# Moving a gate product to the branch stage, other buffer counts in the mixers, one raw weight buffer and another spacing of the convolution pairs in a hybrid decoder layer

## The chip, the cores and the metric

The kernel runs on one core of a Trainium2 chip. A core has the engines PE (TensorE, matrix products), DVE (VectorE), ACT (ScalarE), POOL (GpSimd) and SP (SyncE), which here issues all the DMAs. Each engine runs its own list of instructions in order; semaphores make one wait for another. The metric is the device time of one launch in microseconds (us). Times come from runs, and the profile from one execution of its own.

## The reference

One layer of a decoder with four branches runs over 16 meta tokens, 1024 prompt tokens and 8 samples of 4 tokens, all in float32, 1024 wide:

```
xn = rmsnorm(h)
gq, gk, gv, glr, gg, hq, hf, hi, hg, mq, mk, mv, mi, mf, mo, mg, ca, cb, cg, gate = split(xn @ w_in)
zA = head_rmsnorm(gla(gq, gk, gv, glr)) * silu(gg)
zB = head_rmsnorm(hgrn2(hq, hf, hi))    * silu(hg)
zC = head_layernorm(mlstm(mq, mk, mv, mi, mf) * sigmoid(mo)) * silu(mg)
zD = silu(layernorm(causal_conv31(ca * sigmoid(cb)))) * silu(cg)
mixed = sum_b sigmoid(gate_b) * (z_b @ w_branch[b])
y = rmsnorm(h + mixed @ w_out)
```

Each branch is 512 wide, four heads of 128. Recurrent and convolution states are outputs too.

## The kernel before, in words

A float32 operand of a product is split into a high and a low part (`split_w`: ACT writes `wh`, L138, POOL or DVE writes `wl`, L139), and each product is three matrix products on PE: high by high, low by high, high by low. Raw weights come from HBM into the tile `wraw` (`load_raw`, L132), two buffers in the pool `wp`; `wh` and `wl` have two each.

The program is written in one order, and a planner turns it into a fixed list for each engine. It takes, at each point of a modelled time, the ready instruction that comes first in the program; a tile with all its buffers taken makes the next user wait. So a tile's number of buffers (`bufs`) decides what can run ahead, and the lists were fixed before the chip runs them.

The stages, with their rough times in the profile:

- 0 to 90 us: normalisation, transposition, the first gate projections (`gate_direct`), and sums of x for the next stage (`combine_x`).
- 90 to 500 us: 19 projection pairs. A pair computes two blocks of 128 columns of `xn @ w_in` with seven half-size products instead of eight (`pair`, L252 to L311): r0 and r1 are the two raw weights, DVE and ACT form sums of weights and of results, PE runs 7 x 24 matrix products. Four of the pairs are convolution pairs (`conv_pair`): they write u = ca * sigmoid(cb) into the tile `u`, one buffer (ACT at L349 first). `conv_taps` then runs the 31 taps on DVE (L386, L388) into `y`, one buffer, behind the transposes of the stored convolution state (PE L372, into `u` by ACT L373, small products at L383); `tc.cur_priority = pr + 700` ranks its DVE work behind that of the pairs after it. `conv_states` writes the new state out. The other 15 pairs (`pair_to`) send gates, `cg` and silu(gg), silu(hg), silu(mg), sigmoid(mo) to DRAM (`gscr`, `cscr`, `sscr`). The loop at L457 puts a convolution pair at places 0, 4, 8 and 12 of the 19.
- 500 to 1300 us: the mixers: four HGRN2 heads, two GLA units of two heads, four mLSTM heads. The products over levels of the decay are in the tile `tot`, the running states and some scratch in `sall`, one buffer each; `f` holds the decay, one buffer. 16 further gate blocks (`filler`) are projected here as work for PE. At its end each head calls `z_out` (L702): scale, transpose on PE into PSUM, and a DVE product (L720) of the PSUM result, the norm's weight and the gate, which was loaded from `sscr` into the tile `gt`; then one store to `zscr` (L721).
- 1300 to 1518 us: the branch stage, in the order b = 1, 0, 2, 3. `load_z` (L1140) loads four z of a branch and splits them, for the next branch while the current one runs (for b = 1, ahead of it). For each of eight column blocks, `branch` loads a weight (256 KB), splits it and runs 36 matrix products; DVE multiplies by the gate (L1164), POOL adds to the sum (L1165). During b = 1 the convolution's norm (`conv_norm`) runs as well.
- 1518 to 1621 us: the product with `w_out` and the last norm.

PSUM has three accumulators (`acc`), two buffers for levels and three for all else (`mm`) in the mixers and branches.

Of the kernel before, what the change touches and what calls it, by code (L numbers as in the profile page):

```python
# [12 lines left out]
F32 = mybir.dt.float32  # L13
# [3 lines left out]
AF = mybir.ActivationFunctionType  # L17
ALU = mybir.AluOpType
# [47 lines left out]
def trunk(ctx, tc, hx, w_in, w_sm, w_br, w_out, pk, wgk2, mlb, fnorm, s_gla, s_hg, s_c, s_n, s_m, s_cv,  # L66
# [43 lines left out]
    def col(name, i=0):  # L110
        return pkt[:, PK[name][0] + i:PK[name][0] + i + 1]
# [16 lines left out]

    def load_raw(src, c0, kd=KD):
        raw = pools["wp"].tile([P, KD, P], F32, name="wraw", tag="wraw")  # L130
        src = src if c0 is None else src[:, c0:c0 + P].rearrange("(k p) m -> p k m", p=P)
        DMA.dma_start(raw[:, :kd], src)  # L132
        return raw
# [118 lines left out]
    def pair(c0, c1, c11, c12, c22, c21):  # L252


        wp = pools["gph"]
        r0, r1 = load_raw(w_in, c0), load_raw(w_in, c1)
        b11, b21, b12, b22 = r0[:, :KH], r0[:, KH:], r1[:, :KH], r1[:, KH:]
# [199 lines left out]
    for i in range(4):  # L457
        cu = conv_pair(i)
        pair_to(*todo.pop(0))
        conv_taps(i, *cu)  # L460
        pair_to(*todo.pop(0))
        conv_states(i, *cu)
        pair_to(*todo.pop(0))
    for t in todo:
# [55 lines left out]
    def tl(tag, shape=None, bufs=None, name=None):  # L520
        return mx.tile(shape or [P, NT], F32, name=name or tag, tag=tag, bufs=bufs)
# [66 lines left out]
    def levels(qv, nh, k, f):  # L588

        tot = tl("tot", [P, 1072], 1)  # L590
        atts = [(nxt(attb, "att"), att8b[cnt["att"] % 2]) for _ in range(nh)]
# [109 lines left out]

    def z_out(o, rstd, nw, gate, zi, mu=None):  # L702
        if mu is not None:
            for c in range(9):
                n = csz(c)
                V.tensor_scalar(o[:n, c], o[:n, c], mu[:n, c:c + 1], rstd[:n, c:c + 1], ALU.add, ALU.mult)
        else:
            for a in (0, 4):
                V.tensor_tensor(o[:, a:a + 4], o[:, a:a + 4], rstd[:, a:a + 4].unsqueeze(2).broadcast_to([P, 4, P]),
                                ALU.mult)  # L710
            V.tensor_scalar(o[:TAIL, 8], o[:TAIL, 8], rstd[:TAIL, 8:9], None, ALU.mult)
        for c0, c1 in QUADS:
            n = csz(c0)
            ps = mmt("zt")
            for c in range(c0, c1):
                T.transpose(ps[:, (c - c0) * P:(c - c0) * P + n], o[:n, c, :], ident[:n, :n])
            a = NM if c0 == 0 else 0
            e = (c1 - c0 - 1) * P + n
            t0 = c0 * P + a - NM
            V.scalar_tensor_tensor(gate[:, t0:t0 + e - a], ps[:, a:e], nw, gate[:, t0:t0 + e - a], ALU.mult, ALU.mult)  # L720
        DMA.dma_start(zscr[zi], gate)  # L721

    def rms(os, epss):
        n = len(os)
        sq = tl("sall", [P, 9, P], 1, name="sq")
        ms = tl("ms", [P, 18], 1)
        G.memset(ms, 1.0)
        for i, o in enumerate(os):
            for a in (0, 4):
                S.activation(sq[:, a:a + 4], o[:, a:a + 4], AF.Square)  # L730
                V.tensor_reduce(ms[:, 9 * i + a:9 * i + a + 4], sq[:, a:a + 4], AX.X, ALU.add)
            S.activation(sq[:TAIL, 8], o[:TAIL, 8], AF.Square, accum_out=ms[:TAIL, 9 * i + 8:9 * i + 9])
        ms = ms[:, :9 * n]
        V.tensor_scalar(ms, ms, 1.0 / P, EPS * epss, ALU.mult, ALU.add)
        return rsqrt(ms)

    def filler():
        gate_direct(fill.pop(0), tmp=lambda: tl("gd", [P, 352], 1))

    def linear_unit(uid, qv, nh, k, f, prod, vts, s0, epss, finish, pout, sout):  # L740
# [17 lines left out]
        k9 = split3(xk, 2, "k9", 1, mmt("k9p"))  # L758
        sall = tl("sall", [P, 9, P], 1)
        for c0, c1 in QUADS:  # L760
# [60 lines left out]
    def gla_unit(p):  # L821
# [19 lines left out]
        vts = [vtok("gv", 2 * p + i) for i in range(2)]  # L841
        gates = []
        for i in range(2):
            g = tl("gt", [P, NY], 2)
            DMA.dma_start(g, sscr[2 * p + i])
            gates.append(g)
        s0 = tl("s0", [P, NSEQ, 129], 1)[:, :, 0:P]
        DMA.dma_start(s0, s_gla[:, 2 * p:2 * p + 2].rearrange("b h k v -> (h k) b v"))
        linear_unit(p, qg, 2, k, f, prod, vts, s0, 64.0,
                    lambda i, o, r: z_out(o, r, col("gla_norm"), gates[i], 2 * p + i),  # L850
                    lambda st: DMA.dma_start(p_gla[2 * p:2 * p + 2].rearrange("h k v -> (h k) v"), st),
                    lambda st: DMA.dma_start(o_gla[:, 2 * p:2 * p + 2].rearrange("b h k v -> (h k) b v"), st))

    def hg_unit(h):
# [3 lines left out]
        def evf(ps, t0, n):  # L858
# [11 lines left out]
        vt = vtok("hi", h)  # L870
        g = tl("gt", [P, NY], 2)
# [3 lines left out]
        linear_unit(h % 2, q2, 1, k, f, None, [vt], s0, 1.0,  # L875
                    lambda i, o, r: z_out(o, r, col("hg_norm"), g, 4 + h),
                    lambda st: DMA.dma_start(p_hg[h], st),
# [5 lines left out]
    def row(name, tag="vt", n=4):  # L883
        return tl(tag, [P, 9, 129], n, name=name).rearrange("p a b -> p (a b)")[:, :NT]
# [7 lines left out]
    def ml_rows():  # L892
# [8 lines left out]
        s84 = lambda t: t[:, NP:NT].rearrange("p (s j) -> p s j", j=NDEC)  # L901
        b = row("b", "sall", 1)[0:4]
        segm = tl("prod", [4, NT], 1, name="segm")
# [53 lines left out]
    def ml_unit(h):  # L957
# [12 lines left out]
        to_tok_v(sf, so)  # L970
        g = tl("gt", [P, NY], 2)
        DMA.dma_start(g, sscr[8 + h])
        c0t = tl("s0", [P, NSEQ, 129], 1, name="c0t")
# [5 lines left out]
        DMA.dma_start(inb, rscr[4 + h:5 + h].broadcast_to([P, NT]))  # L979
        dm = tl("sall", [P, 9, 129], 1, name="dm")[:, 0:8, 0:P]  # L980
        dmt = tl("dmt", [TAIL, TAIL], 1)
# [4 lines left out]
        S.activation(dmt, dmt, AF.Exp)  # L986
        sd = tl("tot", [P, 8, P], 1, name="sd")
        for c0, c1 in QUADS[:2]:
# [16 lines left out]
        k9 = split3(xk, 2, "k9", 1, mmt("k9p"), cols9[:, h:h + 1])  # L1005
        call = tl("sall", [P, 9, 129], 1, name="call")
        for a in range(0, 9, 3):
# [54 lines left out]
        G.memset(ms, 1.0)  # L1062
        sq = tl("sall", [P, 9, P], 1, name="sq")
        for n, c1, c2 in ((P, 0, 8), (TAIL, 8, 9)):
# [3 lines left out]
        V.tensor_scalar(ms, ms, 1.0 / P, EPS, ALU.mult, ALU.add)  # L1068
        z_out(hc, rsqrt(ms), col("ml_norm", h), g, 8 + h, mu)

# [69 lines left out]
    def load_z(b):  # L1140
        zs = []
        for k in range(4):
            zr = ztl("zr", 2)
            DMA.dma_start(zr, zscr[4 * b + k])
# [4 lines left out]
            S.activation(zh, zr, AF.Copy)  # L1149
            V.tensor_tensor(zl, zr, zh, ALU.subtract)  # L1150
            zs.append((zh, zl))
        return zs
# [180 lines left out]
```

## Time and profile before

| | |
|---|---|
| median of 3 runs | 1619.72 us (1619.08 to 1622.87) |
| the profiled execution | 1622.92 us, of which the span of its instructions is 1621.1 |
| mean granted PE clock | 0.993 of full speed |
| ACT busy, POOL busy | 527.4 us (33%), 467.0 us (29%) |
| DMA traffic | 176.21 MB, mean 109 GB/s |

In the profile's rows, L138 is line 138 of the kernel; `q<-q,tot` names the tile written and the tiles read; SPq is the queue on which SP issues DMAs. "x19" is a count. A row of waits tells which engine at which line waited for which, the total, how often and the longest. A row of a timeline gives start, duration, engine, line, operation and, in brackets, the idle time before it and what ended that. PEld is the loading of weights into PE, which overlaps its products. A busy PE is not PE at its peak, since its products are pipelined.

### The profile page before, as it was taken

The page shows a single profiled execution, that of the slowest core. Times are in us where ns is not written, and L with a number is a line of the kernel's source. Part 1 is how long each engine was busy: PE and PEld are TensorE (multiplying, and loading weights), DVE is VectorE, ACT ScalarE, POOL GpSimd, SP SyncE. Part 2 cuts the span into 40 slices and gives each one's busy share as a digit, 9 for nine tenths or more (in the row PEclk, how much of TensorE's full clock was granted, in tenths as well). Part 3 has the DMA queues.
Part 4 walks back from the last instruction along what each step waited for, and adds up shares of the span by engine and source line. Part 5 has one row for each costly group of instructions (what it writes and reads, how often), then busy time and mean ns, then how long its engine had stood idle before and what let it go on. Part 6 is the DMA issues. An engine that isn't in the chain of part 4 may idle for free.

```text
span 1621.1 us, 27103 instructions
## 1 busy us (share of the span) xinstructions
PE 1582.3 (98%) x10894; PEld 1529.0 (94%) x10894; DVE 1076.6 (66%) x1900; ACT 527.4 (33%) x1015; POOL 467.0 (29%) x412
## 2 busy tenths in 40 slices
PE   7999999899999999999999999999999999999998
PEld 6999999899999999999999998999999999999886
DVE  7959979899994566454544766585864736744523
ACT  6533342333333333212423212133322235522311
POOL 2222222123223122222122322123322312777300
PEclk9999999999999999999999999999999999999999
DMA  5323333232336213131313123143432277676221
GB/s 195 126 75 110 96 105 87 77 103 84 109 99 200 58 38 106 42 101 47 102 46 106 40 68 104 45 147 109 130 96 70 94 222 231 191 232 205 87 105 58
DMA packets 190561, 176.21 MB, mean 109 GB/s; under 512 B 9260, under 2 KB 164800, under 8 KB 190436
## 3 DMA queue, kind: packets, MB, share of 16 engines
q1 hardware_dynamic: 190436, 174.49, 35.1%
q8 instruction: 85, 1.39, 0.4%
q14 instruction: 40, 0.33, 0.1%
HBM read 122.45 MB, written 52.00 MB: 108 GB/s over the span
## 4 chain that ended last, share of the span: by engine, by line
PE 80%; DVE 14%; DMA 2%; issue 2%; ACT 1%; SPq 0%; DVEq 0%; POOLq 0%; POOL 0%; ACTq 0%
PE acc L185 17%; PE acc L187 17%; PE acc L186 17%; DVE y L388 5%; PE lv L627 4%; PE sa L277 2%; PE sa L278 2%; PE sa L279 2%; PE sc L279 1%; PE sc L278 1%; PE sc L277 1%; PE sd L279 1%; PE sd L278 1%; PE sd L277 1%; DVE wl L139 1%
## 5 line engine op out<-in xcount | busy, mean ns | idle before, releaser
L139 POOL TENSOR_TENSOR wl<-wraw,wh 128x1024 fp32r<-128x1024 f32 (+1 forms) x124 | 272.1, 2196 | 680.4 <-ACT wh L138 671.6
L185 PE MATMUL acc<-xh,wh 128*128 128x352 f32 (+2 forms) x1320 | 435.8, 330 | 2.9 <-ACT vt L534 1.9
L186 PE MATMUL acc<-xl,wh 128*128 128x352 f32 (+2 forms) x1320 | 434.3, 329 | 0.0
L187 PE MATMUL acc<-xh,wl 128*128 128x352 f32 (+2 forms) x1320 | 433.5, 328 | 0.0
L185 PEld LDWEIGHTS acc<-xh,wh 128*128 128x128 f32 x1320 | 249.9, 189 | 6.9 <-ACT vt L534 2.9
L186 PEld LDWEIGHTS acc<-xl,wh 128*128 128x128 f32 x1320 | 249.8, 189 | 2.0 <-issue 0.5
L187 PEld LDWEIGHTS acc<-xh,wl 128*128 128x128 f32 x1320 | 249.7, 189 | 1.7 <-issue 0.2
L138 ACT ACTIVATE wh<-wraw 128x512 fp32r<-128x512 f32 (+1 forms) x125 | 110.5, 884 | 253.7 <-PE acc L186 147.7
L388 DVE SCALAR_TENSOR_TENSOR y<-u,pkt,y 128x1024 f32<-128x1024 f32 x120 | 190.8, 1590 | 0.7
L185 PE MATMUL acc<-zh,wh 128*128 128x352 f32 x384 | 124.5, 324 | 0.5 <-DVE gt L1164 0.4
L186 PE MATMUL acc<-zl,wh 128*128 128x352 f32 x384 | 124.3, 324 | 0.0
L187 PE MATMUL acc<-zh,wl 128*128 128x352 f32 x384 | 124.2, 323 | 0.0
L277 PE MATMUL sa<-xh,wh 128*128 128x268 f32 x304 | 89.0, 293 | 6.5 <-ACT u L349 6.1
L642 DVE TENSOR_TENSOR q<-q,tot 128x256 f32<-128x256 f32 (+3 forms) x96 | 59.4, 619 | 53.9 <-PE lv L627 42.6
L278 PE MATMUL sa<-xl,wh 128*128 128x268 f32 x304 | 88.2, 290 | 0.0
L279 PE MATMUL sa<-xh,wl 128*128 128x268 f32 x304 | 88.1, 290 | 0.0
L1165 POOL TENSOR_TENSOR mix<-mix,gt 128x352 f32<-128x352 f32 x72 | 72.1, 1014 | 30.4 <-DVE gt L1164 25.1
L627 PE MATMUL lv<-q,k 128*128 128x128 f32 (+2 forms) x608 | 74.5, 272 | 2.7 <-DVE att L660 2.5
L627 PEld LDWEIGHTS lv<-q,k 128*128 128x128 f32 (+1 forms) x608 | 71.0, 187 | 4.7 <-issue 3.9
L185 PEld LDWEIGHTS acc<-zh,wh 128*128 128x128 f32 x384 | 72.3, 188 | 1.1 <-DVE gt L1164 1.1
L187 PEld LDWEIGHTS acc<-zh,wl 128*128 128x128 f32 x384 | 72.2, 188 | 0.0
L186 PEld LDWEIGHTS acc<-zl,wh 128*128 128x128 f32 x384 | 72.2, 188 | 0.0
(391 smaller groups left out, 3392.9 us busy)
## 6 DMA issues: line engine op xcount, KB each, us to landing
wraw<-w_in SPq DMA_DIRECT2D x92, 512.0 KB, 4.0
gt<-gscr SPq DMA_DIRECT2D x30, 528.0 KB, 5.0
gscr<-gd SPq DMA_DIRECT2D x60, 176.0 KB, 1.9
zr<-zscr SPq DMA_DIRECT2D x16, 528.0 KB
wraw<-w_br SPq DMA_DIRECT2D x32, 256.0 KB, 2.9
gt<-sscr SPq DMA_DIRECT2D x12, 528.0 KB, 3.6
zscr<-gt SPq DMA_DIRECT2D x12, 528.0 KB, 3.3
sscr<-u SPq DMA_DIRECT2D x16, 268.0 KB, 2.3
```

Source lines behind the costliest of these rows:

```text
L138: S.activation(hi[:, :kd], raw[:, :kd], AF.Copy)
L139: (E or G).tensor_tensor(lo[:, :kd], raw[:, :kd], hi[:, :kd], ALU.subtract)
L185: T.matmul(ps, wh(k), ah(k), start=(i == 0), stop=False)
L186: T.matmul(ps, wh(k), al(k), start=False, stop=False)
L187: T.matmul(ps, wl(k), ah(k), start=False, stop=(i == kd - 1))
L277: T.matmul(out, wh, xa[:, k], start=start and k == 0, stop=False, skip_group_check=True)
L278: T.matmul(out, wh, xb[:, k], start=False, stop=False, skip_group_check=True)
L279: T.matmul(out, wl, xa[:, k], start=False, stop=stop and k == KH - 1, skip_group_check=True)
L388: V.scalar_tensor_tensor(ymain, u[:, NM + j:NM + j + NPR], w(j), ymain, ALU.mult, ALU.add)
L627: T.matmul(out(ps[:rows, c], P), k[:, t0:t0 + rows], moving(t0, P), start=True, stop=True)
L642: V.tensor_tensor(qx[:, :, 1], qx[:, :, 1], pv[r, :, 0:1].broadcast_to([rw, nb, h]), ALU.mult)
L1165: G.tensor_tensor(mixed[j][:, t0:t0 + n], mixed[j][:, t0:t0 + n], gt[:, t0:t0 + n], ALU.add)
```

## The change

- `z_out` no longer multiplies by the gate: ACT copies the transposed block, times the norm's weight, from PSUM to a new tile `zst` (two buffers, 512 wide), and each of the three blocks has a store of its own. The tile `gt` and the 12 gate loads leave the mixers. `load_z` loads the gate (`zg`, one buffer) for the branches 0 to 2, and DVE multiplies it into z.
- `tot` and `sall` have two buffers; the filler's `gd` tile (one buffer) is replaced by `zst`.
- `wraw` has one buffer in `wp`; the second raw weight of a pair has one of its own in the pool `gph`.
- After the states of convolution i come 2, 1, 2, 0 pairs instead of one, which puts the convolution pairs at 0, 5, 9 and 14.

```diff
-    def load_raw(src, c0, kd=KD):
-        raw = pools["wp"].tile([P, KD, P], F32, name="wraw", tag="wraw")
+    def load_raw(src, c0, kd=KD, pool="wp"):
+        raw = pools[pool].tile([P, KD, P], F32, name="wraw", tag="wraw", bufs=1)
...
-        r0, r1 = load_raw(w_in, c0), load_raw(w_in, c1)
+        r0, r1 = load_raw(w_in, c0), load_raw(w_in, c1, pool="gph")
...
         conv_taps(i, *cu)
         pair_to(*todo.pop(0))
         conv_states(i, *cu)
-        pair_to(*todo.pop(0))
+        n = (2, 1, 2, 0)[i]
+        for t in todo[:n]:
+            pair_to(*t)
+        del todo[:n]
...
-        tot = tl("tot", [P, 1072], 1)
+        tot = tl("tot", [P, 1072], 2)
...
-    def z_out(o, rstd, nw, gate, zi, mu=None):
+    def z_out(o, rstd, nw, zi, mu=None):
...
-            V.scalar_tensor_tensor(gate[:, t0:t0 + e - a], ps[:, a:e], nw, gate[:, t0:t0 + e - a], ALU.mult, ALU.mult)
-        DMA.dma_start(zscr[zi], gate)
+            z = tl("zst", [P, 512], 2)[:, :e - a]
+            S.activation(z, ps[:, a:e], AF.Identity, scale=nw)
+            DMA.dma_start(zscr[zi, :, t0:t0 + e - a], z)
...
-        gate_direct(fill.pop(0), tmp=lambda: tl("gd", [P, 352], 1))
+        gate_direct(fill.pop(0), tmp=lambda: tl("zst", [P, 512], 2))
...
-        sall = tl("sall", [P, 9, P], 1)
+        sall = tl("sall", [P, 9, P], 2)
...
-        g = tl("gt", [P, NY], 2)
-        DMA.dma_start(g, sscr[4 + h])
...
             DMA.dma_start(zr, zscr[4 * b + k])
+            if b < 3:
+                zg = ztl("zg", 1)
+                DMA.dma_start(zg, sscr[4 * b + k])
+                V.tensor_tensor(zr, zr, zg, ALU.mult)
```

The gate loads of the GLA and mLSTM units go in the same way, and every other use of `tot` and `sall` (`sd`, `sq`, `b`, `dm`, `call`) has two buffers as well.

More of the change, by code (lines that the diff above doesn't have):

```diff
@@ L719, in z_out @@
             t0 = c0 * P + a - NM
-            V.scalar_tensor_tensor(gate[:, t0:t0 + e - a], ps[:, a:e], nw, gate[:, t0:t0 + e - a], ALU.mult, ALU.mult)
-        DMA.dma_start(zscr[zi], gate)
+            z = tl("zst", [P, 512], 2)[:, :e - a]
+            S.activation(z, ps[:, a:e], AF.Identity, scale=nw)
+            DMA.dma_start(zscr[zi, :, t0:t0 + e - a], z)
     def rms(os, epss):
         n = len(os)
-        sq = tl("sall", [P, 9, P], 1, name="sq")
+        sq = tl("sall", [P, 9, P], 2, name="sq")
         ms = tl("ms", [P, 18], 1)
@@ L841, in gla_unit @@
         vts = [vtok("gv", 2 * p + i) for i in range(2)]
-        gates = []
-        for i in range(2):
-            g = tl("gt", [P, NY], 2)
-            DMA.dma_start(g, sscr[2 * p + i])
-            gates.append(g)
         s0 = tl("s0", [P, NSEQ, 129], 1)[:, :, 0:P]
@@ L849, in gla_unit @@
         linear_unit(p, qg, 2, k, f, prod, vts, s0, 64.0,
-                    lambda i, o, r: z_out(o, r, col("gla_norm"), gates[i], 2 * p + i),
+                    lambda i, o, r: z_out(o, r, col("gla_norm"), 2 * p + i),
                     lambda st: DMA.dma_start(p_gla[2 * p:2 * p + 2].rearrange("h k v -> (h k) v"), st),
@@ L870, in hg_unit @@
         vt = vtok("hi", h)
-        g = tl("gt", [P, NY], 2)
-        DMA.dma_start(g, sscr[4 + h])
         s0 = tl("s0", [P, NSEQ, 129], 1)[:, :, 0:P]
@@ L875, in hg_unit @@
         linear_unit(h % 2, q2, 1, k, f, None, [vt], s0, 1.0,
-                    lambda i, o, r: z_out(o, r, col("hg_norm"), g, 4 + h),
+                    lambda i, o, r: z_out(o, r, col("hg_norm"), 4 + h),
                     lambda st: DMA.dma_start(p_hg[h], st),
@@ L901, in ml_rows @@
         s84 = lambda t: t[:, NP:NT].rearrange("p (s j) -> p s j", j=NDEC)
-        b = row("b", "sall", 1)[0:4]
+        b = row("b", "sall", 2)[0:4]
         segm = tl("prod", [4, NT], 1, name="segm")
@@ L970, in ml_unit @@
         to_tok_v(sf, so)
-        g = tl("gt", [P, NY], 2)
-        DMA.dma_start(g, sscr[8 + h])
         c0t = tl("s0", [P, NSEQ, 129], 1, name="c0t")
@@ L979, in ml_unit @@
         DMA.dma_start(inb, rscr[4 + h:5 + h].broadcast_to([P, NT]))
-        dm = tl("sall", [P, 9, 129], 1, name="dm")[:, 0:8, 0:P]
+        dm = tl("sall", [P, 9, 129], 2, name="dm")[:, 0:8, 0:P]
         dmt = tl("dmt", [TAIL, TAIL], 1)
@@ L986, in ml_unit @@
         S.activation(dmt, dmt, AF.Exp)
-        sd = tl("tot", [P, 8, P], 1, name="sd")
+        sd = tl("tot", [P, 8, P], 2, name="sd")
         for c0, c1 in QUADS[:2]:
@@ L1005, in ml_unit @@
         k9 = split3(xk, 2, "k9", 1, mmt("k9p"), cols9[:, h:h + 1])
-        call = tl("sall", [P, 9, 129], 1, name="call")
+        call = tl("sall", [P, 9, 129], 2, name="call")
         for a in range(0, 9, 3):
@@ L1062, in ml_unit @@
         G.memset(ms, 1.0)
-        sq = tl("sall", [P, 9, P], 1, name="sq")
+        sq = tl("sall", [P, 9, P], 2, name="sq")
         for n, c1, c2 in ((P, 0, 8), (TAIL, 8, 9)):
@@ L1068, in ml_unit @@
         V.tensor_scalar(ms, ms, 1.0 / P, EPS, ALU.mult, ALU.add)
-        z_out(hc, rsqrt(ms), col("ml_norm", h), g, 8 + h, mu)
+        z_out(hc, rsqrt(ms), col("ml_norm", h), 8 + h, mu)
     def ml_nout():
```

## The prediction

> **What bounds the kernel now.** I read the page first, then the waits of TensorE (PE), then busy time in chosen stretches, then the order of instructions around each wait. The page's own lines:
>
> ```profile
> span 1621.1 us, 27103 instructions
> ...
> PE 1582.3 (98%) x10894; PEld 1529.0 (94%) x10894; DVE 1076.6 (66%) x1900; ACT 527.4 (33%) x1015; POOL 467.0 (29%) x412
> ...
> PE   7999999899999999999999999999999999999998
> ...
> DVE  7959979899994566454544766585864736744523
> ...
> DMA  5323333232336213131313123143432277676221
> ```
>
> PE is idle for 1621.1 - 1582.3 = 38.8 us in all, and the change neither removes nor adds a matrix product. So whatever it gains must come from this idle time and from stretches in which PE's clock is reduced. DVE is nearly full in slices 4 to 12 (about 120 to 490 us; a slice is 40.5 us), where the projection pairs run; the DMA engines are fullest near 1320 us, where the branch stage begins. The waits of PE, columns total, times and longest:
>
> ```profile
> PE xt L174 <- DVE ss L165: 8.3, 2, 8.1
> PE sa L277 <- ACT u L349: 6.1, 2, 4.8
> PE lv L627 <- DVE att L660: 2.5, 3, 1.7
> PE sds L817 <- DVE gt L720: 2.1, 1, 2.1
> ...
> PE tta L533 <- ACT vf L576: 1.9, 1, 1.9
> ...
> PE sb L277 <- DVE p L306: 1.0, 1, 1.0
> ```
>
> Three of these touch the diff: the two waits for `u` at L349, the one for L720, and the `sb` wait, which belongs to a late convolution pair. The first stands at the kernel's start and stays. Busy time in five stretches (columns: PE, PEld, DVE, ACT, POOL with counts, granted clock, DMA share, GB/s):
>
> ```profile
> 195.24:216.08 20.84, 20.84 (x168) 20.84 (x169) 12.11 (x22) 9.02 (x17) 4.98 (x3) 1.00 0.47 141
> 292.97:296.60 3.63, 0.00 (x1) 0.00 (x0) 3.59 (x2) 0.00 (x0) 1.97 (x1) 1.00 0.00 0
> 296.70:303.50 6.80, 5.68 (x25) 5.62 (x26) 4.14 (x10) 1.34 (x4) 0.84 (x2) 0.50 0.51 157
> 972.60:976.00 3.40, 3.35 (x11) 3.25 (x12) 3.37 (x7) 0.00 (x0) 0.00 (x0) 0.51 0.98 308
> 1002.00:1006.20 4.20, 1.85 (x14) 1.57 (x13) 4.12 (x11) 1.64 (x3) 1.07 (x5) 1.00 0.12 43
> ```
>
> The first row is one projection pair without taps of a convolution: 168 products, 20.84 us of PE, 12.11 us of DVE. The second and third are the longer wait for `u` and what follows it: nothing runs on PE, then 6.80 us at half clock, which cost 6.8 x 0.5 = 3.4 us more. The fourth follows the L720 wait: half clock again, 1.7 us. The last holds a wait of up to 1.7 us (L660) with the clock at 1.00.
>
> **Convolution pairs at 0, 5, 9, 14 instead of 0, 4, 8, 12.** The tile `u` has one buffer, so a convolution pair may write it (L349) only when the 31 taps of the one before have run on DVE. The rows of the second interval (pairs 4 to 8):
>
> ```profile
> L388 DVE SCALAR_TENSOR_TENSOR y<-u,pkt,y 128x1024 f32<-128x1024 f32 x120 | 190.8, 1590 | 0.7
> 200.28 0.18 DVE L361 TENSOR_TENSOR u<-u,u 128x32 f32<-128x32 f32 x1
> 216.08 0.37 PE L372 MATMUL cvp<-ident,cvT 120*128 120x120 f32 x2
> 218.39 1.59 DVE L383 TENSOR_TENSOR y<-u,pkt 128x248 f32<-128x248 f32 x4
> 292.66 4.68 DVE L388 SCALAR_TENSOR_TENSOR y<-u,pkt,y 128x1024 f32<-128x1024 f32 x2
> 297.38 0.68 ACT L349 ACTIVATE u<-sa 128x268 f32<-128x268 f32 x2 [5.05 <-DVE y L388]
> 297.82 0.59 PE L277 MATMUL sa<-xh,wh 128*128 128x268 f32 x1 [4.85 <-ACT u L349]
> ```
>
> A convolution's taps are 190.8 / 4 = 47.7 us of DVE; with four pairs that is 47.7 + 4 x 12.1 = 96 us of DVE beside 4 x 20.84 = 83 us of PE, with five pairs 108 beside 104. So a fifth pair takes most of the deficit away, but only in the intervals that get it: the first (0 to 5) and the third (9 to 14). The second stays at four pairs. Its trouble also has another part: `u` was complete at 200.46, but the taps began at 218.39, because the transposes of the stored state (L372) stood on PE behind pair 5. The change leaves conv_taps behind the pair that follows, so in the second interval taps again begin one pair late, with three pairs left. Spare DVE time of the first interval cannot be carried over, since the next taps need the next `u`.
>
> So: of the two waits for `u`, the shorter (6.1 - 4.8 = 1.3) goes, as the first interval has 20.8 us more; the 4.85 us with its 3.4 us of half clock are moved by one pair and stay; the `sb` wait of 1.0 in the third interval goes. Sum -2.3. The last interval shrinks from seven pairs to five (14 to 18): 47.7 + 4 x 12.1 = 96 us of DVE stand beside 83 us of PE, so the last taps run on for about 13 us into the mixers. There PE multiplies ready weights (11.7 us each, estimated as 72 products at the 0.16 us start to start of the rows 1429.69 and 1429.85 below), and the evacuation of the first projection is on ACT; I cost it at nothing, 0 to 5 us if that cover fails.
>
> **Gate product out of z_out.**
>
> ```profile
> L720 DVE SCALAR_TENSOR_TENSOR gt<-zt,pkt,gt 128x496 f32<-128x496 f32 (+2 forms) x36 | 19.1, 577 | 15.9 <-PE zt L716 15.8
> 967.69 0.60 ACT L534 ACTIVATE vt<-tta 128x512 f32<-128x512 f32 x1
> 967.82 2.63 DVE L642 TENSOR_TENSOR q<-q,f 64x256 f32<-64x256 f32 x2 [1.36 <-PE lv L627]
> 971.89 1.54 DVE L720 SCALAR_TENSOR_TENSOR gt<-zt,pkt,gt 128x496 f32<-128x496 f32 x3
> 972.65 0.79 PE L817 MATMUL sds<-vb,k 96*128 96x512 f32 x1 [2.14 <-DVE gt L720]
> ```
>
> 36 operations, 19.1 us, leave DVE; ACT gets 36 of at most 0.60 us (the L534 copy of 512 columns), about 20 us, and is busy for a third of the span. The one time that PE paid was at 970.5: L720 stood behind L642 and the mask copies on DVE while it held the PSUM buffer that `sds` needed. ACT was free there after 968.3. I take the 2.1 us and the 1.7 us of half clock as gone: -3.8. [...] The row 972.60:976.00 shows 0.51 right behind a wait of 2.14 us, so the measurement decides and I take 3.8.
>
> z now goes out in three stores instead of one, 24 more on the SP queue; none is waited for before the branch stage. The twelve gate loads leave the mixers.
>
> **Two buffers for tot and sall.** The remaining waits in the mixers (2.5 for L660, 1.9 for `vf`) stand at unit boundaries behind the tile `f`, which keeps one buffer. I give the buffers nothing; a new order of the units may win or lose, bounded by those 4.4 us either way.
>
> **Gates multiplied in load_z.** Twelve loads of 528 KB and twelve DVE products enter the branch stage. For the first branch (b = 1), nothing else has to be waited for but these:
>
> ```profile
> 1304.56 0.86 SPq L1144 DMA_DIRECT2D zr<-zscr  x2
> 1308.35 1.09 ACT L1149 ACTIVATE zh<-zr 128x1056 fp32r<-128x1056 f32 x1
> 1317.97 1.26 DVE L1150 TENSOR_TENSOR zl<-zr,zh 128x1056 fp32r<-128x1056 f32 x1 [1.26 <-ACT zh L1149]
> 1323.40 0.41 PE L185 MATMUL acc<-zh,wh 128*128 128x352 f32 x1
> 1320.00:1360.00 40.00, 40.00 (x260) 39.89 (x259) 22.77 (x40) 20.15 (x43) 9.82 (x9) 1.00 0.82 243
> ```
>
> Today the fourth z is split at 1319.23, 4.2 us before PE needs the first. One load takes 1308.35 - 1304.56 = 3.8 us, a product 1.26 (as zl). zg has one buffer, so load and product follow each other: 4 x (3.8 + 1.26) = 20 us from 1304.6, then zh and zl, 2.4 us: 1327.2. PE needs the fourth z after nine products (1.4 us), at 1324.9: 2.3 us late. With an earlier start of the loads it is nothing. Bounds 0 and 6; I take 1.5. Later branches have 45 us and more for it. The other eight products are 10 us on a DVE that is 57% busy here; they hold up the evacuation by perhaps 0.5 in all (0 to 2).
>
> **One raw weight buffer.** In the pairs nothing changes: r0 and r1 had a buffer each and have one each now. In the direct projections and the branches the next load waits for the split of the weight before:
>
> ```profile
> wraw<-w_br SPq DMA_DIRECT2D x32, 256.0 KB, 2.9
> gt<-gscr SPq DMA_DIRECT2D x30, 528.0 KB, 5.0
> ...
> 1424.17 0.63 ACT L138 ACTIVATE wh<-wraw 128x512 fp32r<-128x512 f32 x1 [0.61 <-PE acc L186]
> 1424.88 1.28 POOL L139 TENSOR_TENSOR wl<-wraw,wh 128x512 fp32r<-128x512 f32 x1 [0.86 <-ACT wh L138]
> 1429.69 0.33 PE L187 MATMUL acc<-zh,wl 128*128 128x352 f32 x1
> 1429.85 0.32 PE L185 MATMUL acc<-zh,wh 128*128 128x352 f32 x1
> 1429.93 0.63 ACT L138 ACTIVATE wh<-wraw 128x512 fp32r<-128x512 f32 x1 [5.13 <-PE acc L186]
> ```
>
> A branch weight lasts 1429.93 - 1424.17 = 5.76 us on PE. The new loop is split (1424.17 to 1426.16, 2.0) plus 0.1 plus load (2.9) = 5.0 us, and the split ends 1429.85 - 1426.16 = 3.7 us before PE needs it. So the loop closes with 0.8 us to spare for each weight: cost 0, as long as a load lands within 3.7 us. What waits behind such a load on SP are gt, zr and zg. At the start of the kernel the second weight is loaded up to 4 us later; there PE waits for DVE anyway (the 8.3 above), cost 0.
>
> **Sum.** -1.3 - 1.0 - 2.1 - 1.7 + 1.5 + 0.5 = -4.1 us. The profiled execution took 1622.9 us (span 1621.1) and would take 1618.8; it is 3.2 above the median of the runs shown, 1619.7, from which the forecast is 1615.6. About 0.3% (4.9 us) is what a measurement of this kernel can tell from no change.
>
> **Rivals.**
> First: the long wait for `u` goes as well. It needs the transposes of the second convolution's state to be placed ahead of pair 6, so that its taps start with the full interval. For it: `u` is free earlier than today. Against: at 216.08 they stood exactly behind the pair that precedes them in the program. 4.85 + 3.4 = 8.3 more: 1607.3. Chance 0.22.
> Second, on the other side: the raw loop becomes the bound in the first two branches. DMA is 82% busy there and the change adds eight loads of 528 KB from that point on; if w_br loads then land after 4.6 us (between 2.9 and the 5.0 of gt), the loop is 6.7 us against 5.76: 16 x 0.9 = 15 less the 3.7 of slack, 11 us; at 5.0, 17. It decides from 3.7 us on. Result 1626 to 1632, at the middle 1626.6. Against: 2.9 is the median of just these loads in this stage. Chance 0.18.
> Third: the planner orders the mixers anew and puts waits of the sort of L660 or `vf`, with half clock behind them, where none was: two more of 1.9 + 1.7 are +7, so 1622.8. Every unit is touched, which speaks for it; PE always has a projection to turn to, which speaks against. Chance 0.15.
>
> **How the numbers follow.** Forecast 0.45, with its own range 1610 to 1621: it counts 0.18 as faster and 0.27 as the same. The first rival is faster (0.22), the second slower (0.18), the third 0.01 faster, 0.06 the same, 0.08 slower. Faster 0.41, same 0.33, slower 0.26. The range reaches below the first rival by the 4.4 us of the mixers (1603) and to the upper price of the second (1632).
>
> **What would show it.** Pairs: PE waits for L349 once, not twice, for about 4.8 us near 314 us, with 0.50 clock behind it; if there is no such wait, the first rival holds. L720 appears on ACT, and no `sds` wait for it. Branch stage: ACT's wh at L138 released by PE, not by the load; if by wraw again and again, the second rival holds. zh of the fourth z within 3 us of PE's first zh product. The forecast is wrong if PE's idle time falls by over 10 us or rises.

## The result, and the profile after

The changed kernel takes 1662.47 us (median of 4 runs, 1660.18 to 1666.55); the kernel before took 1620.56 on the same chip (4 runs). The ratio is 1.026, 95% interval 1.0236 to 1.0284: slower by 42 us, where 4 us faster was forecast, and outside the range. The profiled execution took 1663.02 us, at a mean granted clock of 0.986 instead of 0.993. Of all the runs below, two single executions (3958 us of no_zg, 4500 us of d_sall) lie far above all others and are left out. The page:

```profile
span 1661.2 us, 27148 instructions
...
PE 1595.7 (96%) x10894; PEld 1535.9 (92%) x10894; DVE 1079.8 (65%) x1876; ACT 549.6 (33%) x1051; POOL 457.7 (28%) x412
...
PE   6999999899998999999998999999999999999998
...
DMA  5323333233343112221313022143323289575331
```

PE has the same 10894 products, but is idle for 1661.2 - 1595.7 = 65.5 us instead of 38.8, and busy for 13.4 us more with the same products, at the lower mean clock (0.986 against 0.993). The DMA row has 8 and 9 where the branch stage begins (slices 33 and 34) instead of 7 and 7. The waits of PE after (total, times, longest):

```profile
PE lv L630 <- DVE tot L602: 5.3, 1, 5.3
PE sa L277 <- ACT u L349: 5.1, 2, 4.8
PE xt L174 <- DVE xl L179: 4.0, 1, 4.0
PE acc L185 <- DVE q L543: 3.9, 1, 3.9
...
PE acc L185 <- ACT zst L217: 2.4, 1, 2.4
PE lvt L634 <- DVE k L646: 2.0, 1, 2.0
PE acc L187 <- POOL wl L139: 1.9, 2, 1.0
PE acc L185 <- ACT wh L138: 1.9, 2, 1.7
...
PE sds L821 <- DVE vb L701: 1.8, 2, 1.0
```

The wait of `sds` for L720 is gone, as forecast, and the short wait for `u` has shrunk from 1.3 to 0.3 us. In their place stands a list of new ones: for level products (`tot`, and `k` behind them), for `zst`, for `q`, and for raw weights. Stretches of the changed kernel (PE, PEld, DVE, ACT, POOL, granted clock, DMA share, GB/s):

```profile
317.74:322.57 4.83, 0.00 (x1) 0.00 (x1) 4.69 (x3) 0.45 (x2) 2.07 (x2) 0.98 0.00 0
322.60:326.00 3.40, 3.40 (x16) 3.40 (x17) 1.00 (x3) 0.81 (x3) 0.72 (x1) 0.52 0.91 274
909.50:919.80 10.30, 5.25 (x20) 5.28 (x21) 10.11 (x21) 1.54 (x3) 6.72 (x20) 0.50 0.19 51
1360.00:1400.00 40.00, 38.17 (x243) 37.18 (x242) 33.26 (x50) 20.27 (x43) 9.21 (x8) 1.00 0.96 317
```

The first two rows are the long wait for `u`, where and as it was forecast. The third holds a wait in the mixers that was not there before, with 10.2 us of half clock that begin in it; the last is the first branch with its DMA engines 96% busy (0.82 from 1320 to 1360 us before).

To place the loss I cut each trace at four points: PE's first product of the pairs, its last of the pairs, its first branch product and its last. All stage times below (us) are differences of these points, each of the one profiled execution of its kernel; they add up to its span but for rounding.

| kernel | head | pairs | mixers | branch | tail | span |
|---|---|---|---|---|---|---|
| before | 89.8 | 410.8 | 822.8 | 194.4 | 103.4 | 1621.1 |
| after | 94.3 | 406.2 | 847.9 | 209.6 | 103.2 | 1661.2 |

So the head lost 4.5, the pairs gained 4.6, the mixers lost 25.1 and the branch stage 15.2.

### The profile page after: what moved, and what is told of

It reads as the page before. It is cut to its first block, busy times and chain, and to the rows that moved or that the text cites. A ratio compares the mean times of both kernels' runs of the same rounds, so it can differ in the third digit from the quotient of the medians.

```text
span 1661.2 us, 27148 instructions
## 1 busy us (share of the span) xinstructions
PE 1595.7 (96%) x10894; PEld 1535.9 (92%) x10894; DVE 1079.8 (65%) x1876; ACT 549.6 (33%) x1051; POOL 457.7 (28%) x412
## 5 line engine op out<-in xcount | busy, mean ns | idle before, releaser
L139 POOL TENSOR_TENSOR wl<-wraw,wh 128x1024 fp32r<-128x1024 f32 (+1 forms) x124 | 266.2, 2147 | 731.4 <-ACT wh L138 678.7
L645 DVE TENSOR_TENSOR q<-q,tot 128x256 f32<-128x256 f32 (+3 forms) x96 | 53.6, 559 | 55.5 <-PE lv L630 44.2
L630 PE MATMUL lv<-q,k 128*128 128x128 f32 (+2 forms) x608 | 75.3, 274 | 6.6 <-DVE tot L602 5.3
L630 PEld LDWEIGHTS lv<-q,k 128*128 128x128 f32 (+1 forms) x608 | 71.9, 189 | 8.6 <-issue 6.9
```

The costliest lines, as they stand in the source:

```text
L139: (E or G).tensor_tensor(lo[:, :kd], raw[:, :kd], hi[:, :kd], ALU.subtract)
L630: T.matmul(out(ps[:rows, c], P), k[:, t0:t0 + rows], moving(t0, P), start=True, stop=True)
L645: V.tensor_tensor(qx[:, :, 1], qx[:, :, 1], pv[r, :, 0:1].broadcast_to([rw, nb, h]), ALU.mult)
```

## The experiments

The parts of the change are called spacing, raw buffer, gate edit (z_out, load_z and `zst`) and two buffers (`tot` and `sall`). Some of them fit in memory only together, so they are partly tested alone and partly in a chain.

**a_spacing** is the kernel before with the spacing alone.

```diff
-        pair_to(*todo.pop(0))
+        n = (2, 1, 2, 0)[i]
+        for t in todo[:n]:
+            pair_to(*t)
+        del todo[:n]
```

> The kernel before with the new places of the convolution pairs alone (0, 5, 9, 14). Theory: the pair stage gains the 4.7 us that it gained in the changed kernel (410.8 to 406.2 us), but the last taps run on into the mixers, where PE then waits as in the changed kernel (1.75 and 3.87 us plus half clock, 7.7 us up to the first level product). Net +3 us: about 1623. Rival: the waits at the mixers' start come from the buffers and not from the spacing; then the 4.7 us are all there is, about 1616.

Measured: 1628.57 us, ratio 1.0041 (1.0027 to 1.0055). Pairs 406.9 (-3.9), mixers 832.4 (+9.6). Its waits of PE behind the last pair:

```profile
PE acc L185 <- DVE q L543: 4.0, 1, 4.0
...
PE acc L185 <- ACT k L863: 1.8, 1, 1.8
...
PE acc L185 <- DVE p L306: 1.5, 1, 1.5
```

They stand at 523, 509 and 499 us, with 3.4 us of half clock behind the last in time. On DVE the taps now run past the final pair:

```profile
505.72 9.90 DVE L388 SCALAR_TENSOR_TENSOR y<-u,pkt,y 128x1024 f32<-128x1024 f32 x6
515.54 0.46 DVE L864 TENSOR_SCALAR f<-f,lbt 128x358 f32<-128x358 f32 x1
```

PE's last product of the pairs ends at 495.5 us, the last tap 20 us later, and DVE's first work for the mixers (L864) stands right behind it. The mixers lose more than twice what the pairs gain.

**b_raw** is the kernel before with one raw buffer alone.

```diff
-        raw = pools["wp"].tile([P, KD, P], F32, name="wraw", tag="wraw")
+        raw = pools[pool].tile([P, KD, P], F32, name="wraw", tag="wraw", bufs=1)
-        r0, r1 = load_raw(w_in, c0), load_raw(w_in, c1)
+        r0, r1 = load_raw(w_in, c0), load_raw(w_in, c1, pool="gph")
```

> The kernel before with one raw weight buffer alone. Theory (the raw loop bounds the branch stage by itself): 4.5 us at the start (first pair at 94 instead of 90 us) and 8 to 12 us in the branch stage, though no gate is loaded there: about 1634. Rival (the added gate loads made the branch stage longer, the one buffer alone closes its loop as the sum of split 2.0 and load 2.9 said): 4.5 us at the start alone, about 1625.

Measured: 1633.69 us, ratio 1.0071 (1.0056 to 1.0086). Head 93.6 (+3.8), branch 202.0 (+7.6), mixers unchanged (822.5). So the raw buffer costs 11.5 us of span by itself.

**two_half** is the changed kernel with the branch weights, which fill half a raw tile, loaded into its two halves by turns.

```diff
-        bh, bl = load_w(w_br[b * 512:(b + 1) * 512], j * P, 4)
+        raw = rawb[:, 4 * (j % 2):4 * (j % 2) + 4]
+        DMA.dma_start(raw, w_br[b * 512:(b + 1) * 512][:, j * P:j * P + P].rearrange("(k p) m -> p k m", p=P))
+        bh, bl = split_w(raw, 4)
```

> The changed kernel, but in the branch stage the raw tile's two halves (a branch weight fills one) are used in turn, so that a weight is loaded ahead again; all before that stage is as in the changed kernel. Theory (raw loop): most of the 15.2 us that the branch stage lost come back, about 1650, and the first split of a weight is again released by PE. Rival (traffic of the gate loads): the stage stays at about 210 us, 1660 or more.

**no_zg** is the changed kernel without the gate loads and products of load_z, so its output lacks the gates of the branches 0 to 2; **two_half_no_zg** has both edits and lacks the same.

```diff
-            if b < 3:
-                zg = ztl("zg", 1)
-                DMA.dma_start(zg, sscr[4 * b + k])
-                V.tensor_tensor(zr, zr, zg, ALU.mult)
```

> Changed kernel without the gate loads and gate products of the branch stage: the gates of branches 0 to 2 are left out of the output. The branch stage took 194.4 us before, 202.0 with one raw buffer alone, 209.6 in the changed kernel, and 205.4 in it with the branch weights alternating between halves of the raw tile. Theory that the losses are two and add up (single raw buffer about 7.6 us, gate loads and products about 7.6 us): branch stage 200 to 204 us, span about 1653 us. Rival that the single raw buffer alone makes the late weights and the gate loads only ride along: branch stage 207 to 211 us, span about 1660 us.

> Changed kernel with both suspects of the branch stage gone: no gate loads or products (the gates of branches 0 to 2 are left out of the output), and the branch weights alternate between the two halves of the raw tile. Theory that these two hold the whole loss of the branch stage: 193 to 196 us as before, span about 1646 us. Rival that something else does (the z tiles stored later in the mixers, or the clock): 200 us or more, span 1652 us or more.

| kernel | us | branch stage |
|---|---|---|
| after | 1662.47 | 209.6 |
| two_half | 1661.74 | 205.4 |
| no_zg | 1657.63 | 201.7 |
| two_half_no_zg | 1651.91 | 194.7 |

The first expectation of two_half failed: the raw loop is worth only 4.2 us while the gates are loaded. Without them it is worth 7.0, and the gate loads and products, which no run takes apart, are worth 7.9 with the raw loop and 10.7 without. With both gone the stage is back at 194.7 us (before: 194.4), so nothing else is lost there. These differences are those of the branch stage and not of the time: PE has the same order of products up to that stage in all four kernels, and yet their mixers took 847.9, 850.9, 850.9 and 851.2 us, with 27.3 us of half clock in the first and 34.1 in the others. A difference of some 3 us between the mixers of two executions can therefore be the clock alone.

With one buffer a load is issued only when the split before it is through, so that whatever delays a split also delays the next load. The trace of the changed kernel shows two kinds of such a delay in the first branch; first SP's queue, then ACT's, then POOL's and PE's rows:

```profile
1368.57 0.38 SPq L132 DMA_DIRECT2D wraw<-w_br  x1
...
1384.52 0.38 SPq L132 DMA_DIRECT2D wraw<-w_br  x1
1385.63 0.33 SPq L1139 DMA_DIRECT2D zr<-zscr  x1
1386.50 0.33 SPq L1199 DMA_DIRECT2D gt<-gscr  x1
1388.36 0.32 SPq L1142 DMA_DIRECT2D zg<-sscr  x1
...
1393.20 0.45 SPq L132 DMA_DIRECT2D wraw<-w_br  x1
```

```profile
1373.99 0.63 ACT L138 ACTIVATE wh<-wraw 128x512 fp32r<-128x512 f32 x1 [5.49 <-DMA wraw<-w_br]
...
1390.47 0.62 ACT L138 ACTIVATE wh<-wraw 128x512 fp32r<-128x512 f32 x1
...
1398.94 1.51 ACT L1127 ACTIVATE yc<-yb,pkt 128x128 f32<-128x128 f32 x4 [4.93 <-PE yb L1125]
1400.32 0.64 ACT L138 ACTIVATE wh<-wraw 128x512 fp32r<-128x512 f32 x1
```

```profile
1391.17 1.79 POOL L139 TENSOR_TENSOR wl<-wraw,wh 128x512 fp32r<-128x512 f32 x1 [6.67 <-ACT wh L138]
```

```profile
1401.01 0.43 PE L185 MATMUL acc<-zh,wh 128*128 128x352 f32 x1 [1.68 <-ACT wh L138]
```

The load issued at 1368.57 lands late: ACT waits for it until 1373.99, 5.42 us after its issue, and PE still has products of the weight before. The second kind costs PE time. POOL ends a split at 1392.96, the next load is issued at 1393.20, and ACT begins the next split only at 1400.32, 7.1 us later; but the row ahead of it shows ACT waiting 4.93 us for PE's `yb` and not for the load, whose own landing these rows do not show. ACT's list has L1127 ahead of the split, and PE stands for 1.68 us. In the whole stage 18 of the 32 splits are released by their load, 2.8 to 5.4 us after its issue; in b_raw, where no gate is loaded, it is 19, 2.8 to 4.8 us after. PE's waits for `wh` and `wl` in the changed kernel, 1.9 us each in the rows above, come near to what two_half wins back.

**no_a** is the changed kernel with the old spacing; **b_c** has the raw buffer and the gate edit, but one buffer each for `tot` and `sall`.

```diff
-        n = (2, 1, 2, 0)[i]
-        for t in todo[:n]:
-            pair_to(*t)
-        del todo[:n]
+        pair_to(*todo.pop(0))
```

> The changed kernel with the old places of the convolution pairs (0, 4, 8, 12). Theory: the pair stage loses its 4.7 us again and the mixers' start gains 7.7, so about 1659; the other 17 us of the mixers stay, being from the new order of the units. Rival: the late start of the mixers upset the later units too, and most of the 25 us go: about 1642.

```diff
-        tot = tl("tot", [P, 1072], 2)
+        tot = tl("tot", [P, 1072], 1)
-        sall = tl("sall", [P, 9, P], 2)
+        sall = tl("sall", [P, 9, P], 1)
```

> Kernel before with one raw buffer and the gates moved to the branch stage; old convolution spacing, level products and states in one buffer. The mixers (from the last of the pairs to the first branch product) took 822.8 us before, 822.5 with the raw buffer alone, 847.9 in the changed kernel and 844.3 in the changed kernel with the old spacing. Theory that the gate edit (a ScalarE copy and a shared staging tile in place of a product in place) holds most of the mixers' loss: mixers 838 to 846 us, span about 1657 us, and the waits of TensorE for the staging tile are there, those for the level products with two buffers (5.3 us) are not. Rival that the two buffers of level products and states reorder the mixers for the worse: mixers 821 to 827 us, span about 1640 us. Branch stage in both 205 to 212 us.

Measured: no_a 1662.42 us (1.0248, 1.0232 to 1.0263), b_c 1642.96 us (1.0138, 1.0114 to 1.0161). The mixers take 844.3 us in no_a and 818.3 in b_c. My theory, that the gate edit and its shared staging tile held the mixers' loss, falls: with them alone the mixers are 4.2 us faster than with the raw buffer alone (822.5). In the mixers the two buffers lose 26.0 us, in the time 19.5.

**d_tot** and **d_sall** are b_c with two buffers for one of the two tiles.

```diff
-        tot = tl("tot", [P, 1072], 1)
+        tot = tl("tot", [P, 1072], 2)
```

> Kernel before with one raw buffer, the gates moved to the branch stage and two buffers for the level products alone (the chunk states keep one). The mixers took 818.3 us with one buffer of each and 844.3 with two of each; there the products of the fifth unit began at 815 instead of 852 us and those of the sixth at 905 instead of 954 us, before the unit ahead was through its levels. Theory that the second buffer of level products lets the planner start a unit's levels inside the unit ahead, so that TensorE stands behind products and gates that are not ready: mixers 838 to 848 us, span about 1661 us, the wait of 5.3 us for the level products and half-clock stretches there. Rival that the second buffer of the states does it: mixers 817 to 823 us, span about 1640 us.

```diff
-        sall = tl("sall", [P, 9, P], 1)
+        sall = tl("sall", [P, 9, P], 2)
```

> Kernel before with one raw buffer, the gates moved to the branch stage and two buffers for the chunk states and squares alone (the level products keep one). Theory that the second buffer of level products holds the mixers' loss: mixers 816 to 822 us, as with one buffer of each (818.3), span about 1640 us. Rival that the second buffer of the states holds it: mixers 838 to 848 us, span about 1661 us. If both carry a part, the two parts add up to about 26 us.

Measured: d_tot 1648.54 us, mixers 832.0 (+13.7 over b_c); d_sall 1646.32 us, mixers 825.4 (+7.1). Neither holds it alone: 13.7 + 7.1 = 20.8 of the 26.0 in the mixers come from the single tiles, and the rest of 5.2, not much above what the clock alone can do, appears only when both have two. In the time the parts add up less well: +5.6 and +3.4 for the single tiles, +19.5 for both, because the branch stage is 6.6, 6.1 and 4.1 us shorter than in b_c. There b_c has an order of PE's products of its own, and the other three have one in common; why is left open. The waits are told apart cleanly. Of d_tot:

```profile
PE lv L627 <- DVE tot L599: 5.3, 1, 5.3
...
PE lvt L631 <- DVE k L643: 2.0, 1, 2.0
```

and of d_sall:

```profile
PE acc L185 <- ACT zst L217: 2.1, 1, 2.1
...
PE sds L818 <- DVE vb L698: 1.8, 2, 1.0
...
PE n0p L948 <- ACT zst L721: 1.6, 1, 1.6
```

All five stand in the changed kernel and none in b_c at this size. For `sall` the waits are all that is sure: d_sall's executions, 1642.3 to 1649.2 us, overlap with those of b_c, 1642.3 to 1647.7, and the profiled one was the shortest of them. How `tot` does it is seen in when its products run (count, shortest, median and longest in ns, first and last start). Of b_c:

```profile
L599 DVE TENSOR_TENSOR tot<-f x6: 701/705/717, 521.0 to 953.9; 128x536 f32<-128x536 f32 x6
```

and of no_a:

```profile
L599 DVE TENSOR_TENSOR tot<-f x6: 705/712/718, 519.4 to 905.2; 128x536 f32<-128x536 f32 x6
```

The sixth unit's products start at 905.2 instead of 953.9 us, and the fifth's at 815.3 instead of 852.4. It is the buffer of `tot` that moves them, as the rows of d_tot and then of d_sall show:

```profile
L599 DVE TENSOR_TENSOR tot<-f x6: 699/706/720, 519.1 to 900.3; 128x536 f32<-128x536 f32 x6
L599 DVE TENSOR_TENSOR tot<-f x6: 698/708/1006, 517.7 to 953.7; 128x536 f32<-128x536 f32 x6
```

With one buffer a unit's products had to wait until the unit ahead was through with `tot` (in b_c its last reader, on POOL, ends at 852.4, where the fifth unit's products start); that held the units apart. With two, the planner starts a unit's levels inside the unit ahead, and PE meets them before DVE has the factors. The worst place in the changed kernel, on DVE and then on POOL:

```profile
906.94 0.72 DVE L602 TENSOR_TENSOR tot<-f 128x536 f32<-128x536 f32 x1 [1.16 <-ACT f L832]
907.69 0.44 DVE L602 TENSOR_TENSOR tot<-tot 128x268 f32<-128x268 f32 x1
908.04 4.62 DVE L645 TENSOR_TENSOR q<-q,tot 64x256 f32<-64x256 f32 x2
912.68 0.53 DVE L646 TENSOR_TENSOR k<-k,tot 128x256 f32<-128x256 f32 x1
913.13 1.27 DVE L663 COPY_PREDICATED att<-lvm,lv 128x256 f32<-128x256 uint8 x2
914.21 0.32 DVE L602 TENSOR_TENSOR tot<-tot 128x130 f32<-128x130 f32 x1
```

```profile
907.93 2.41 POOL L139 TENSOR_TENSOR wl<-wraw,wh 128x1024 fp32r<-128x1024 f32 x1 [1.98 <-ACT wh L138]
...
910.35 2.03 POOL L783 TENSOR_TENSOR o<-vt,dg 128x1024 f32<-128x1024 f32 x1
```

PE has nothing from 909.21 to 914.55 (the 5.3), and the half clock in and behind it is the third row of the stretches above. By the granted clock the mixers have no half-clock time in b_c, 20.5 us in d_tot, 3.4 in d_sall, 30.7 in no_a, 27.3 in the changed kernel and 6.8 before. In no_a 5.9 of the 30.7 us fall into time in which PE is idle anyway; the rest costs, as an estimate from the clock of 0.5, 24.8 / 2 = 12.4 us, beside 21.4 - 7.8 = 13.6 us more of idle PE than in b_c. The sum, 26.0, is what the stage lost: the clock took nearly as much as the waits.

**z_aph** and **z_pri** try to have the gate edit's gain in the mixers without its loss in the branch stage. The first computes the gate product on ACT and POOL in the mixers; the second only gives it a later place in the planner's order.

```diff
-            V.scalar_tensor_tensor(gate[:, t0:t0 + e - a], ps[:, a:e], nw, gate[:, t0:t0 + e - a], ALU.mult, ALU.mult)
+            for x0 in range(a, e, 256):
+                x1 = min(x0 + 256, e)
+                z = tl("gd", [P, 352], 1)[:, :x1 - x0]
+                S.activation(z, ps[:, x0:x1], AF.Identity, scale=nw)
+                gv = gate[:, t0 + x0 - a:t0 + x1 - a]
+                G.tensor_tensor(gv, gv, z, ALU.mult)
```

> Kernel before, its gates kept in the mixers and its buffers as they were; only the gate product is taken off VectorE: ScalarE copies the transposed output with its norm out of PSUM in parts of at most 256 columns, GpSimd multiplies the gate in SBUF. Theory that the gain of the gate edit in the mixers (822.8 to 818.3 us with the raw buffer) is the z product that stood on VectorE ahead of what the state matmuls need, and that the branch stage's loss comes only from the raw buffer and the gate loads there: mixers 817 to 820 us, branch stage 194 to 195 us, span 1616 to 1619 us, 0.1 to 0.3 per cent faster than the kernel before. Rival that the gain came from the gates' loads and buffers leaving the mixers: mixers 822 us or more, time the same or longer.

```diff
+            pr = tc.cur_priority
+            tc.cur_priority = pr + 300
             V.scalar_tensor_tensor(gate[:, t0:t0 + e - a], ps[:, a:e], nw, gate[:, t0:t0 + e - a], ALU.mult, ALU.mult)
+            tc.cur_priority = pr
```

> Kernel before, with the gate product given a later place in the planner's order (300 steps later) and nothing else changed. Same theory as for the product on ScalarE and GpSimd: if VectorE takes what the state matmuls need first, the wait of 2.14 us and the half-clock stretch behind it go, mixers 818 to 820 us, span 1616 to 1619 us. Rival: the product comes later, holds its PSUM bank longer and the next transposes wait instead, mixers 822 us or more.

Both missed. z_aph: 1643.42 us (1.0137, 1.0123 to 1.0151), mixers 843.5, because PE now meets one transpose too early:

```profile
PE zt L716 <- DVE o L709: 10.6, 1, 10.6
```

z_pri: 1621.56 us (0.9999, 0.9989 to 1.001); the `sds` wait of 2.1 us is still there, so the place given did not move the product past what it holds up. z_aph thus makes the mixers 20.7 us slower, with 10.6 us of one wait and 23.9 us of half clock in and behind it, where the gate edit itself gained 4.2. Its order of instructions differs from that of the kernel before, but what put the transpose there was not traced further.

**a_0_4_9_13** is the kernel before with the pairs at 0, 4, 9 and 13 and one left at the end.

```diff
-        pair_to(*todo.pop(0))
+        n = (1, 2, 1, 1)[i]
+        for t in todo[:n]:
+            pair_to(*t)
+        del todo[:n]
```

> Kernel before with the pairs spaced 0, 4, 9, 13, then one more at the end (one, two, one and one pairs after the four intervals) in place of one after each interval and two at the end. The changed spacing alone gained 4 us in the pairs' stage (the second long wait for u) and lost 9.6 us at the start of the mixers, where taps now ran over. Theory that the loss comes from the taps that are pushed past the last pair: with one pair left behind the last taps instead of none, the pairs' stage is near 407 us as with the changed spacing and the mixers 823 to 826 us, span 1617 to 1620 us. Rival that any pair taken from the end costs what it brings in: mixers 828 us or more, span 1622 us or more.

Measured: 1623.88 us (1.0008, 0.9999 to 1.0018). The last tap now ends 2 us before PE's last product of the pairs, and the mixers are at 820.0 us, so the loss of a_spacing does come from taps past the last pair; but the pairs stay at 412.7, because the long wait for `u` is now at 401 us and 7.5 us long. That left open what this wait hangs on. **taps_first** and **taps_first_0_4_9_13** issue a convolution's taps ahead of the gate pair that follows it, on the spacing before and on this one.

```diff
+        conv_taps(i, *cu)
         pair_to(*todo.pop(0))
-        conv_taps(i, *cu)
         conv_states(i, *cu)
```

> Kernel before with the taps of each convolution issued ahead of the gate pair that follows it, so that the state transposes stand one pair (about 21 us) earlier on TensorE; spacing and all else as before. Theory that the long wait for u (4.85 us at 293 us, with half-clock stretches of 6.8 us there) hangs on the late start of the taps of the second convolution: they start near 202 us instead of 218, end near 280 instead of 296, the wait goes, and the pairs' stage takes about 402 to 404 us instead of 410.8, the span 1612 to 1615 us, ratio about 0.995. Rival that the spacing decides: the wait stays within 1 us of 4.85 and the time is within 0.2 per cent of the kernel before.

> The same move with pairs at 0, 4, 9, 13, then one more at the end, where the wait for u was 7.49 us at 401 us and the pairs' stage 412.7 us. Theory of the late start: the taps of the third convolution start near 308 us instead of 325 and end by 388, the wait of 7.49 us and its 10.2 us of half clock go, pairs' stage 399 to 402 us, span 1608 to 1612 us. Rival that the spacing decides: a wait of 5 us or more stays, the time is within 0.2 per cent of that spacing without the move.

Measured: 1620.57 us (0.9989, 0.998 to 0.9998) and 1619.50 us (0.9986, 0.9976 to 0.9996). In taps_first, around the second convolution and the next write of `u`:

```profile
192.83 0.37 PE L372 MATMUL cvp<-ident,cvT 120*128 120x120 f32 x2
...
203.71 1.39 DVE L383 TENSOR_TENSOR y<-u,pkt 128x248 f32<-128x248 f32 x4
...
281.88 0.68 ACT L349 ACTIVATE u<-sa 128x268 f32<-128x268 f32 x2 [5.01 <-DVE y L388]
...
282.33 0.39 PE L277 MATMUL sa<-xh,wh 128*128 128x268 f32 x1 [1.77 <-ACT u L349]
```

The transposes stand at 192.83 instead of 216.08, the taps begin at 203.71 instead of 218.39, and the long wait of 4.85 becomes 1.77, with no half clock behind it; in the other spacing the 7.5 become 3.3. So the wait does hang on the late transposes, and the theory holds for the wait. It does not for the time: the pairs of taps_first take 409.9 us, 0.9 less instead of 7 to 9. PE comes to the next write of `u` at 280.6 us instead of 293.0, and to the one after at 368.5, and finds the taps just short of their end each time: three waits for `u` of 4.6 us in all stand where two of 6.1 stood. Other small waits grew (PE is idle for 8.9 us of the pairs, against 9.3), and the rest of the shortfall was not traced. Moved into the other spacing, 6.5 us of the pairs are gained (406.2 against 412.7) and 4.4 lost in the mixers (824.4 against 820.0). About 1.5 of these are lost at the start of the mixers; the rest stands behind the waits for `vf` and `sds`, where two stretches of 3.4 us at half clock appear that a_0_4_9_13 does not have. These two are the only kernels with the whole work that are faster than the two kernels compared here, by 0.11 and 0.14% against the kernel before, less than the 0.3% that I took as the bound.

## Why the prediction was wrong, point by point

Undone one after the other, the profiled spans give the account: before 1621.1; raw buffer +11.5; gate edit +8.1 (mixers -4.2, branch stage +12.2); two buffers +20.4 (mixers +26.0, branch stage -4.1, which I did not follow up); spacing +0.1. Sum 40.1 us.

- *Two buffers: "I give the buffers nothing; ... bounded by those 4.4 us either way".* This is the largest failed step: +26.0. The bound was taken from waits that stood there, as if a buffer could only remove or lengthen those. It changes what the planner may place where. The third rival had the mechanism (new waits, with half clock behind them) and put it at +7, "two more of 1.9 + 1.7"; there were more waits, up to 5.3 us long, and 27.3 us of half clock (30.7 in no_a). "PE always has a projection to turn to" was wrong here: the order is fixed before the run, and PE stood for 5.3 us in front of the one product that came next.
- *One raw buffer: cost 0, "as long as a load lands within 3.7 us".* It cost 11.5: 7.6 in the branch stage and 3.8 in the head. The second rival had the mechanism and the limit of 3.7 us, but not the reason: it needed the gate loads, and b_raw has none there. That its price was 11 is luck, since it counted the branch stage alone, which lost 7.6 without the gates and 4.2 beside them. I chose the median of 2.9 us "of just these loads in this stage", a median taken while they were issued ahead. In b_raw nine of the 19 loads that a split waited for took longer than 3.7 us, up to 4.8; and the loop of split plus load left out what stands ahead of the split in ACT's list. In the head, "PE waits for DVE anyway" failed too: the wait for `xl` at L179 grew from 1.9 to 4.0 us. The heads of the seven kernels with two raw buffers take 88.4 to 90.5 us, those of the nine with one 93.3 to 95.1.
- *Gates in load_z: +1.5 and +0.5.* The +1.5 for the fourth z of the first branch is nearly there: PE waits 1.6 us for `zh`. The rest is mis-sized. Without loads and products the stage is 7.9 us shorter, or 10.7 with the raw loop mended. I had priced the products on DVE and the first z, not what twelve loads of 528 KB may do to the weight loads among them at 96% DMA share; as loads and products were taken out together, it is not shown which of them costs it.
- *Gate product out of z_out: -2.1 and -1.7.* Right for the wait: in b_c the mixers gain 4.2, and the `sds` wait for that product is gone. The 1.7 of half clock, and that 4.2 is so near to 3.8, are partly luck. Both half-clock stretches of the mixers vanish in b_c, also the one behind the wait for `vf`, which still stands there with 1.83 us; and a_0_4_9_13 keeps the `sds` wait of 2.14 us and has no half clock behind it (below).
- *Spacing: -1.3 and -1.0, and "0 to 5 us if that cover fails".* The pairs gain 3.9 where 2.3 was forecast. The overrun of the taps was forecast as 13 us and is 20 (515.6 against 495.5 in a_spacing); it was priced at nothing, and the mixers lost 9.6 with the spacing alone, twice my upper bound. Beside the rest of the change they lost 3.6 (847.9 - 844.3), which is no more than the clock alone can do.
- *The long wait stays.* Right: 4.83 us at 317.74, clock 0.52 behind it, though for 3.4 us and not 6.8. The first rival falls for this change. The reading that late transposes cause the wait was right too (taps_first); that its 8.3 us would all come back was not.

The sign of the forecast hung on four costs set to nothing: the second buffers, the raw loop in the branches, the raw buffer in the head, and the overrun of the taps. The runs show a cost for each of the four.

## What to carry to other kernels

Where a planner lays out the order, a second buffer is a permission to reorder, not a gift: read where the tile's first write stands afterwards, and time it alone. A transfer time measured while there is slack is no price for a loop without slack; price the loop with the longer landing times of the same loads, and with what stands ahead of its first step in that engine's list. When a step is costed at zero, price what happens if its cover fails, and add those prices up before choosing a sign.

## What the runs showed of the hardware

VectorE's level products took 2.0 us in the median, instead of 0.42, while GpSimd ran a product of its own. Those of L642 in the kernel before (shortest, median and longest in ns):

```profile
L642 DVE TENSOR_TENSOR q<-q,tot x96: 405/424/2525, 546.8 to 1034.0; 128x256 f32<-128x256 f32 x36, 64x256 f32<-64x256 f32 x36, 128x264 f32<-128x264 f32 x8, 64x264 f32<-64x264 f32 x8
```

Of the products of L642 and L643, the 169 that hardly overlap a GpSimd product take 423 ns in the median and 492 at most; the 17 that lie under one for more than half their time take 2044 in the median, up to 2525 (two of them only 418). Under small copies and fills of GpSimd they were not longer: 22 of the 169 lie under such for more than half their time and take 405 to 451. In the rows at 908.04 two of them take 4.62 us and end within 0.3 us of the ends of POOL's two products (910.34 and 912.38). At 0.42 each they would have taken 0.84, so 3.8 of the 5.3 us that PE lost there come from this; that share is an estimate from the rows and not tested by a run. Why they take longer was not shown.

The stretches of half clock in the kernels before and after are 3.41, 6.83 or 10.24 us long, the ones at the kernel's end (5.49 and 6.23) aside. Half clock came behind waits shorter than that: behind 1.86 us at 891 and 2.14 at 970 in the kernel before, but not behind 1.83 us at 895 in b_c, nor behind the same wait of 2.14 us in a_0_4_9_13:

```profile
974.07 0.50 PE L820 MATMUL sds<-vb,k 96*128 96x512 f32 x1 [2.14 <-DVE gt L723]
974.07:977.50 3.43, 3.43 (x20) 3.39 (x21) 3.39 (x7) 0.00 (x0) 0.00 (x0) 1.00 0.82 275
```

The traces tell the two apart. In the kernel before, the stretches begin at 23.65, 296.71, 894.04 and 972.55 us, which are 80, 175 and 23 steps of 3.413 us apart; in the changed kernel the ten stretches begin 87, 61, 86, 25, 25, 5, 26, 75 and 88 such steps apart. The 2.14 us of the kernel before lie with 2.04 us in the one step that ends at 972.55; in a_0_4_9_13 they fall into two steps, with 1.56 and 0.58 us. In the traces of the kernels before and after, divided into such steps from 40 us to the last branch product, the steps at full clock in which PE was idle longest were followed by half clock: three in the kernel before, with 3.41, 2.04 and 1.86 us, and seven in the changed one, with 1.85 to 3.41 us. Of the others, with at most 1.22 us of idle PE before and 1.68 after, one was followed by it: the step at 1008.50 us of the changed kernel, which holds products of only two columns (`dg`, L750) that the rows count as 2.02 us of busy PE. At half clock the level products of 128 columns start 0.21 us apart (L630 after, 1013.20 to 1014.48 us), at full clock 0.11 (L627 before, 1010.85 to 1011.51 us). So the wait of 2.14 us was followed by 3.41 us of half clock in one kernel, 1.7 us more as an estimate from the 0.51 granted there, and by none in another, and any change ahead of such a wait can move it.
